# Two-layer hybrid trunk on one core: the feed-forward up projections as Strassen 2x2 block products, the down projection in five parts

## Chip, core and metric

One core of one Trainium2 chip (trn2). The time is the device time of one execution in microseconds (us), the median of the runs shown.

## What is computed

The trunk has two layers on 512 tokens of width D = 1024, and each layer has two feed-forward sublayers (FF = 2816) with a mixer sublayer between them. Four times, therefore, the kernel computes a gated feed-forward step:

```python
def rmsnorm(x, g):
    y = xf * lax.rsqrt(jnp.mean(xf * xf, axis=-1, keepdims=True) + EPS)
    return (y * g).astype(x.dtype)
def swiglu(x, w13, w2):
    g, u = jnp.split(x @ w13, 2, axis=-1)
    return (jax.nn.silu(g) * u) @ w2
...
for l in range(DEPTH):
    x = x + 0.5 * swiglu(rmsnorm(x, ffn1_norm[l]), ffn1_w13[l], ffn1_w2[l])
    h = rmsnorm(x, mix_norm[l])
    ...
    x = x + merged @ w_out[l]
    x = x + 0.5 * swiglu(rmsnorm(x, ffn2_norm[l]), ffn2_w13[l], ffn2_w2[l])
return rmsnorm(x, final_norm)
```

The mixer sublayer (pooling, mLSTM, differential attention) is the same in both kernels.

## The kernel before, in words

Activations are stored feature-major: `x` is 8 tiles of 128 features x 512 tokens. A matmul has a 128x128 weight block as its stationary operand and up to 512 token columns moving past it. Inputs are float32, and each product is made of three matmuls on rounded halves (`k3`, L217, lines L220 to L222): high x high, high x low, low x high. So one output block of an up projection (128 columns of w13, 8 blocks of K) takes 8 x 3 = 24 matmuls of 128x512, and a column pair (gate g and up u) takes 48.

**Weights.** `weight()` (L202) hands out the next weight tile. It is loaded by a DMA on SP's queue (`load_weight`, up to 128x1024 numbers), its high half is cast on ACT (L198) and its low half is a subtract on DVE (L199). The raw tile has 3 buffers, the halves 2 each; loads run two tiles ahead and splits one.

**A feed-forward layer** (`ffn`, L497). The 22 column pairs come in three `PARTS` of 8, 7 and 7. A pair is two blocks, g then u. When g is done, `take_g` multiplies by the norm factor R on DVE (L507) and applies Silu on ACT (L508). When u is done, `take_u` multiplies by R on DVE (L511), forms u*g on POOL (L512), casts the high half on ACT (L514) and subtracts the low half on DVE (L515). After each part come 8 down blocks, one for each 128 output features: as many k steps as the part has pairs, then an update of x on DVE (L531). In the last part each updated x tile is also prepared for the next norm by `prep` (L305): ACT and DVE make `xh` and `xl` = x times the gain, split in halves (L319, L320), ACT squares x (L332) and POOL adds the squares up (L333).

**The norm.** `norm()` (L352) runs beside the first blocks of the stage that follows. It sums the squares over features on PE (L349), takes the power -1/2 on POOL (L341), spreads the result on PE (L371) and copies it to R on ACT (L361). Blocks that end before R is there keep their results in PSUM until R comes (`self.later`).

**Other pieces.** `tables()` (L411 to L494) makes the cosine and sine tables for the mixer, some 25 DVE and some ACT operations on 128x512 tiles; it is issued as `extra` of the very first feed-forward layer, right after its first part's pairs, before the first 8 down blocks. The last layer ends with `finish` (L1041): the last part's down blocks in two halves of 256 token columns, each with its own sum of squares and final norm.

**Order of work.** PE's order is the order in which the program is written (`manual_schedule` for PE). For DVE, ACT, POOL and SP a scheduler fixes one static order in advance; each engine then works through its queue strictly in that order. `weave` (L280) mixes a second generator (norm, mixers) into PE's stream by an estimated clock; `defer` puts a piece of work at a later point of that clock.

```python
PARTS = ((0, 8), (8, 15), (15, 22))
...
    for m in range(KD):
        def take(ps, m=m):
            nc.vector.scalar_tensor_tensor(
                out=self.x[m], in0=ps, scalar=0.5, in1=self.x[m], op0=ALU.mult, op1=ALU.add
            )
            if last:
                self.prep(m, gnext)
        yield from self.fm(act, take)
```

## Time and profile before

| | |
|---|---|
| median of 3 runs | 2309.61 us (2306.61 to 2311.46) |
| profiled execution | 2309.4 us, its span 2307.6 us, mean granted clock 0.992 |
| PE (matmul) busy | 2269.6 us, 98% of the span, 10740 matmuls |
| DVE / ACT / POOL busy | 1236.2 us (54%) / 802.5 us (35%) / 339.5 us (15%) |
| DMA | 220.59 MB, mean 96 GB/s |

The span runs from the first to the last recorded instruction of one profiled execution; 1.8 us of its 2309.4 us lie outside the span. PE's busy share says how much of the span a matmul was in flight. The order of work decides which of the other engines' operations PE waits for, and the list of PE's waits names them.

### The profile page before, as it was taken

How to read it: one execution, taken by the hardware profiler on the slowest of the kernel's cores; microseconds unless marked ns; L12 is line 12 of the kernel's file. 1: busy time of each engine (PE TensorE's matmuls, PEld its weight loads, DVE VectorE, ACT ScalarE, POOL GpSimd, SP SyncE). 2: the span in 40 equal slices, each digit the busy share in tenths (PEclk: the TensorE clock that was granted, in tenths of full speed). 3: DMA queues.
4: the chain of work that ended last, by engine and by line, in shares of the span. 5: the costliest groups of instructions: out<-in, count | busy, mean ns of one | idle time of the engine just before them, and what ended most of it. 6: DMA issues, size and time to landing. Idle time of an engine off the chain costs nothing.

```text
span 2307.6 us, 26698 instructions
## 1 busy us (share of the span) xinstructions
PE 2269.6 (98%) x10740; PEld 1881.1 (82%) x10740; DVE 1236.2 (54%) x1594; ACT 802.5 (35%) x1181; POOL 339.5 (15%) x251
## 2 busy tenths in 40 slices
PE   8999999999999999999999999999999999999998
PEld 6888888887887888888888888888877878888888
DVE  5564455668547454444444444466776564545355
ACT  3332234534353322222332222354334533323234
POOL 3101012012004210101210010110120042101013
PEclk9999999999999999999999999999999999999999
DMA  4333333323222233333333333332322323333334
GB/s 144 103 101 95 97 94 90 102 78 95 86 83 84 90 101 94 98 94 98 97 95 97 95 91 101 92 96 89 92 87 78 87 87 93 99 94 95 100 94 140
DMA packets 67277, 220.59 MB, mean 96 GB/s; under 512 B 8233, under 2 KB 10809, under 8 KB 67153
## 3 DMA queue, kind: packets, MB, share of 16 engines
q1 hardware_dynamic: 64432, 215.86, 31.2%
q10 hardware_dynamic: 2496, 2.43, 0.3%
q8 instruction: 84, 1.38, 0.2%
q0 software_dynamic: 224, 0.60, 0.1%
q14 instruction: 41, 0.33, 0.0%
HBM read 212.55 MB, written 2.11 MB: 93 GB/s over the span
## 4 chain that ended last, share of the span: by engine, by line
PE 88%; DVE 5%; POOL 3%; issue 2%; ACT 2%; DMA 0%; POOLq 0%; SPq 0%; ACTq 0%; DVEq 0%
PE mm L220 28%; PE mm L221 28%; PE mm L222 27%; POOL t L1026 2%; DVE wl L199 1%; PE mx L141 1%; PE mx L138 1%; PE mx L971 1%; PE mx L871 1%; PE mx L541 1%; DVE t L1022 1%; POOL t L512 1%; ACT wh L198 1%; DVE A L562 0%; ACT A L1028 0%
## 5 line engine op out<-in xcount | busy, mean ns | idle before, releaser
L220 PE MATMUL mm<-xh,wh 128*128 128x512 f32 x2080 | 821.8, 395 | 2.0 <-ACT wh L198 1.3
L221 PE MATMUL mm<-xl,wh 128*128 128x512 f32 x2080 | 811.4, 390 | 2.7 <-DVE xl L320 2.6
L222 PE MATMUL mm<-xh,wl 128*128 128x512 f32 x2080 | 812.0, 390 | 0.5 <-DVE wl L199 0.5
L198 ACT CAST wh<-wr 128x1024 fp32r<-128x1024 f32 (+2 forms) x406 | 417.8, 1029 | 1091.5 <-PE mm L221 556.8
L199 DVE TENSOR_TENSOR wl<-wr,wh 128x1024 fp32r<-128x1024 f32 (+2 forms) x406 | 585.7, 1443 | 81.8 <-ACT wh L198 77.3
L221 PEld LDWEIGHTS mm<-xl,wh 128*128 128x128 f32 x2080 | 391.4, 188 | 84.3 <-DVE xl L320 5.9
L222 PEld LDWEIGHTS mm<-xh,wl 128*128 128x128 f32 x2080 | 391.2, 188 | 83.8 <-DVE wl L199 1.3
L220 PEld LDWEIGHTS mm<-xh,wh 128*128 128x128 f32 x2080 | 391.5, 188 | 82.9 <-DVE xh L317 1.9
L220 PE MATMUL mm<-A,wh 128*128 128x512 f32 (+1 forms) x888 | 336.8, 379 | 8.4 <-ACT A L1028 6.8
L221 PE MATMUL mm<-A,wh 128*128 128x512 f32 (+1 forms) x888 | 336.9, 379 | 1.8 <-DVE A L515 1.6
L222 PE MATMUL mm<-A,wl 128*128 128x512 f32 (+1 forms) x888 | 336.2, 379 | 0.6 <-DVE wl L199 0.6
L512 POOL TENSOR_TENSOR t<-t,t 128x512 f32<-128x512 f32 x88 | 119.8, 1361 | 1143.5 <-ACT wh L198 974.8
L511 DVE TENSOR_TENSOR t<-mm,R 128x512 f32<-128x512 f32 x88 | 60.9, 692 | 284.2 <-PE mm L222 284.2
L220 PEld LDWEIGHTS mm<-A,wh 128*128 128x128 f32 x888 | 168.9, 190 | 40.4 <-ACT A L1028 7.6
L221 PEld LDWEIGHTS mm<-A,wh 128*128 128x128 f32 x888 | 169.0, 190 | 35.3 <-DVE A L515 3.8
L222 PEld LDWEIGHTS mm<-A,wl 128*128 128x128 f32 x888 | 168.8, 190 | 31.9 <-DVE wl L199 1.5
L531 DVE SCALAR_TENSOR_TENSOR x<-mm,x 128x512 f32<-128x512 f32 x88 | 60.8, 691 | 215.7 <-PE mm L222 215.7
L507 DVE TENSOR_TENSOR t<-mm,R 128x512 f32<-128x512 f32 x88 | 60.9, 692 | 162.9 <-PE mm L222 147.9
L514 ACT CAST A<-t 128x512 fp32r<-128x512 f32 x88 | 54.8, 622 | 119.9 <-POOL t L512 119.9
L333 POOL TENSOR_TENSOR ssq<-ssq,t 128x512 f32<-128x512 f32 x42 | 70.8, 1685 | 158.8 <-ACT t L332 158.3
L220 PE MATMUL mm<-wh,xh 128*128 128x256 f32 (+1 forms) x256 | 73.7, 288 | 4.2 <-DVE mif L591 2.6
L221 PE MATMUL mm<-wl,xh 128*128 128x256 f32 (+1 forms) x256 | 72.5, 283 | 0.0
(202 smaller groups left out, 1622.7 us busy)
## 6 DMA issues: line engine op xcount, KB each, us to landing
wr<-in_w13a SPq DMA_DIRECT2D x88, 512.0 KB, 3.6
wr<-in_w13b SPq DMA_DIRECT2D x88, 512.0 KB, 3.6
wr<-in_w_fm SPq DMA_DIRECT2D x76, 512.0 KB, 3.6
wr<-in_w2b SPq DMA_DIRECT2D x40, 448.0 KB, 3.3
wr<-in_w2a SPq DMA_DIRECT2D x32, 448.0 KB, 3.3
wr<-in_w2a SPq DMA_DIRECT2D x16, 512.0 KB, 3.7
wr<-in_w_p SPq DMA_DIRECT2D x16, 512.0 KB, 3.5
wr<-in_w_out SPq DMA_DIRECT2D x16, 512.0 KB, 3.5
```

The costliest lines, as they stand in the source:

```text
L198: self.last_hi = nc.scalar.copy(hi, raw)
L199: self.last_lo = nc.vector.tensor_tensor(out=lo, in0=raw, in1=hi.bitcast(F32), op=ALU.subtract)
L220: nc.tensor.matmul(ps, wh, xh, start=start, stop=False)
L221: nc.tensor.matmul(ps, wh, xl, start=False, stop=False)
L222: nc.tensor.matmul(ps, wl, xh, start=False, stop=stop)
L333: nc.gpsimd.tensor_tensor(out=self.ssq, in0=self.ssq, in1=sq, op=ALU.add)
L507: nc.vector.tensor_tensor(out=g, in0=ps, in1=self.R, op=ALU.mult)
L511: nc.vector.tensor_tensor(out=u, in0=ps, in1=self.R, op=ALU.mult)
L512: self.last_pool = nc.gpsimd.tensor_tensor(out=u, in0=u, in1=g, op=ALU.mult)
L514: nc.scalar.copy(ah, u)
L531: nc.vector.scalar_tensor_tensor(out=self.x[m], in0=ps, scalar=0.5, in1=self.x[m], op0=ALU.mult, op1=ALU.add)
L1026: nc.gpsimd.tensor_tensor(out=acc, in0=acc, in1=t, op=ALU.add)
```

## The change

The 22 pairs come in five parts of 5, 5, 4, 4 and 4. The first part's 5 pairs are computed as before. The other 17 pairs of each layer (68 in all four) are computed as a 2x2 block product: K in two halves of 512, the tokens in two halves of 256 (`H`), and the two "rows" of the block are the pair's g and u columns. Instead of 8 products of half blocks there are 7, each 4 k steps x 3 = 12 matmuls of 128x256: 84 matmuls of 128x256 take the place of 48 of 128x512.

The operands of the 7 products are combinations. On the token side `operands(k)` makes x times gain times R (here R is multiplied in before the matmul), the differences t1 to t4 and their high and low halves, all on DVE and ACT, in four calls per layer that come 1, 8, 15 and 22 us of the estimated clock after R. On the weight side `split_weight` makes sums and differences of the raw halves of g and u on DVE (forms f2, f3, f4; f1 is u's raw first half), then splits them as before. The products run in the order a, c, d, b (`pair_a` to `pair_b`); each half result is copied out of PSUM on ACT or added to a copy on DVE, and u*g of these pairs is on DVE (it stays on POOL in the 5 plain pairs). `gated` makes the activation's halves as L514 and L515 did.

The 8 down blocks of part p-1 (5 or 4 k steps each) are laid between the pieces of part p's pairs, in an order that `ffn_plan` sets; the last part's own 8 follow at the end (or the two halves of `finish`). `tables()` is issued where the plan has "x", ahead of the first layer's last 8 down blocks.

Memory changes with it: weights share a ring "w" of 7 tiles, the forms have 7 tiles "V", down weights have tiles "dr", "dh", "dl" of their own, "A" grows from 24 to 52 buffers and takes over xh, xl, y, dv and the squares; pools with a phase replace t2, t4 and mv. Weights are loaded up to 16 us ahead by estimated PE time, and split up to 7 us ahead.

The diff, cut to its core:

```diff
-PARTS = ((0, 8), (8, 15), (15, 22))
+PARTS = ((0, 5), (5, 10), (10, 14), (14, 18), (18, 22))
+H = T // 2
+MM = 0.2268
+def ffn_plan(end):
+    plan = [("u", 0, j) for j in range(*PARTS[0])]
...
+    for p in range(1, n):
+        f0, f1 = PARTS[p]
+        rest = [("D", p - 1, m) for m in range(KD)]
+        tail = [rest.pop() for _ in range(2)][::-1] if p == n - 1 else []
+        slots = 2 * (f1 - f0) - 1
+        put = [[] for _ in range(slots + 1)]
+        for i, d in enumerate(rest):
+            put[1 + i * slots // len(rest)].append(d)
+        for i, j in enumerate(range(f0, f1)):
+            plan += [("a", p, j)] + ([("b", p, j - 1)] if j > PARTS[1][0] else []) + put[2 * i]
+            plan += [("c", p, j)] + put[2 * i + 1] + [("d", p, j)]
+        if p == n - 1:
+            plan += [("b", p, f1 - 1)] + tail
+    plan.append(("x", 0, 0))
+    plan += [("E", n - 1, h) for h in range(2)] if end else [("D", n - 1, m) for m in range(KD)]
+    return plan
...
+            if kind == "f2":
+                raw = src["s"] = self.wtile()
+                add(raw[:, q1], g[:, q1], g[:, q2], ALU.add)
+                add(raw[:, q2], raw[:, q1], u[:, q1], ALU.subtract)
+            elif kind == "f3":
+                raw = u
+                add(u[:, q1], u[:, q1], g[:, q1], ALU.subtract)
+            else:
+                raw = g
+                add(g[:, q1], u[:, q2], src["s"][:, q2], ALU.subtract)
+            hi, lo = self.forms_tile(), self.forms_tile()
+            self.split(hi, lo, raw)
...
+    def operands(self, k, gcol):
...
+            nc.vector.scalar_tensor_tensor(out=xn[:, q], in0=self.x[i], scalar=g, in1=self.R, op0=ALU.mult, op1=ALU.mult)
...
+        for o, a, b in ((t1, b12, b11), (t2, b22, t1), (t3, b22, b12), (t4, b21, t2)):
+            nc.vector.tensor_tensor(out=o, in0=a, in1=b, op=ALU.subtract)
+        v = self.act(dt=F32R)
+        X["b11"][k] = v[:, :H], v[:, H:]
+        self.split(v[:, :H], v[:, H:], b11, False)
+        for src, names in ((xn[:, q2], ("b21", "b22")), (t[:, q1], ("t1", "t2")), (t[:, q2], ("t3", "t4"))):
+            hi, lo = self.act(dt=F32R), self.act(dt=F32R)
+            self.split(hi, lo, src, False)
...
+    def block(self, ps, w, name, start=False):
+        for k, x in enumerate(self.X[name]):
+            self.k3(ps, (w[0][:, k, :], w[1][:, k, :]), x, start and k == 0, k == 3, True)
+            yield 1.5 * MM
+    def gated(self, u, g, act):
+        ah, al = self.act(dt=F32R), self.act(dt=F32R)
+        nc.scalar.copy(ah, u)
+        nc.vector.tensor_tensor(out=al, in0=u, in1=ah.bitcast(F32), op=ALU.subtract)
...
+    def pair_a(self):
+        p = {"a": self.ps("mx")[:, :H], "b": self.ps("mx")[:, :H], "u": self.act(), "g": self.act()}
+        w = self.weight()
+        yield from self.block(p["a"], w, "b11", start=True)
+        nc.scalar.copy(p["u"][:, :H], p["a"])
+        hi, lo = self.weight()
+        yield from self.block(p["b"], (hi[:, 0:4, :], lo[:, 0:4, :]), "t1", start=True)
+        nc.scalar.copy(p["g"][:, H:], p["b"])
...
+    def pair_b(self, p, act):
+        yield from self.block(p["a"], p["a22"], "t4")
+        u, g = p["u"], p["g"]
+        self.last_silu = nc.scalar.activation(g[:, :H], p["a"], AF.Silu)
+        nc.vector.tensor_tensor(out=u, in0=u, in1=g, op=ALU.mult)
+        self.gated(u, g, act)
+    def pair_c(self, p):
+        yield from self.block(a, p["s2"], "t2")
+        nc.scalar.copy(p["u"][:, H:], a)
+        hi, lo = self.weight()
+        ps = self.ps()[:, :H]
+        yield from self.block(ps, (hi[:, 4:8, :], lo[:, 4:8, :]), "b21", start=True)
+        nc.vector.tensor_tensor(out=p["u"][:, :H], in0=p["u"][:, :H], in1=ps, op=ALU.add)
...
+    def pair_d(self, p):
+        yield from self.block(a, p["s3"], "t3")
+        nc.vector.tensor_tensor(out=g[:, H:], in0=g[:, H:], in1=a, op=ALU.add)
+        self.last_silu = nc.scalar.activation(g[:, H:], g[:, H:], AF.Silu)
+        hi, lo = self.weight()
+        yield from self.block(p["b"], (hi[:, 4:8, :], lo[:, 4:8, :]), "b22")
+        nc.vector.tensor_tensor(out=u[:, H:], in0=u[:, H:], in1=p["b"], op=ALU.add)
+        p["a22"] = hi[:, 4:8, :], lo[:, 4:8, :]
...
-            if extra is not None:
-                extra()
-                extra = None
...
+            elif kind == "x":
+                if extra is not None:
+                    extra()
```

The order of the work at two places, as the two kernels' queues have it.

ACT's queue in the first feed-forward layer, around the end of a plain pair. Before (`t2_72` is u of a plain pair, `wh` high halves of weights):

```order
L198 CAST wh_78_365<-wr_73_330 128x1024
L508 ACTIVATE t2_71_328<-t2_71_328 128x512
L198 CAST wh_86_404<-wr_77_363 128x1024
L514 CAST A_81_396<-t2_72_329 128x512
L198 CAST wh_90_437<-wr_85_402 128x1024
L508 ACTIVATE t2_83_400<-t2_83_400 128x512
L198 CAST wh_98_476<-wr_89_435 128x1024
```

With the change (`V_133` holds g and u of the fifth plain pair, `mx_147` and `mx_148` are the first two half results of the first Strassen pair, `w_...` and `V_...` weights and forms):

```order
L264 CAST V_139_605<-w_136_574 128x512
L662 ACTIVATE V_133_569<-V_133_569 128x512
L264 CAST V_141_611<-w_140_608 128x1024
L264 CAST V_151_653<-w_136_574 128x1024
L264 CAST V_158_707<-w_137_576 128x1024
L651 CAST A_145_644<-V_133_569 128x512
L677 COPY A_149_650<-mx_147_648 128x256
L680 COPY A_150_651<-mx_148_649 128x256
L264 CAST V_161_725<-w_155_661 128x512
L264 CAST V_164_762<-w_163_759 128x1024
L697 COPY A_149_650<-mx_147_648 128x256
```

Before, only casts of later weights and the next pair's Silu stand behind the cast of a pair's gated result (L514). Now the two copies out of PSUM (L677, L680) of the first Strassen pair stand behind that cast (L651) in the same queue.

DVE's queue around `tables()`. Before, between two updates of x at the end of the first part (`y_...` are the tables' tiles):

```order
L463 TENSOR_SCALAR y_154_788<-y_153_785 128x512
L464 TENSOR_SCALAR y_154_788<-y_154_788 128x512
L467 SCALAR_TENSOR_TENSOR y_153_785<-y_154_788,y_153_785 128x512
L463 TENSOR_SCALAR y_155_789<-y_153_785 128x512
L474 TENSOR_SCALAR y_156_790<-y_154_788 128x512
L464 TENSOR_SCALAR y_155_789<-y_155_789 128x512
L531 SCALAR_TENSOR_TENSOR x1_2_69<-mm_167_858,x1_2_69 128x512
L199 TENSOR_TENSOR wl_170_887<-wr_164_852,wh_169_886 128x1024
L467 SCALAR_TENSOR_TENSOR y_153_785<-y_155_789,y_153_785 128x512
```

With the change, at the end of the first feed-forward layer (`A_576` to `A_580` are the tables' tiles, L440 makes xl for the mixer stage, L741 updates x, L265 makes a low half of down weights):

```order
L440 SCALAR_TENSOR_TENSOR A_595_3587<-x1_8_78,vec_15_85,A_594_3586 128x512
L612 SCALAR_TENSOR_TENSOR A_579_3510<-A_580_3511,A_579_3510 128x512
L440 SCALAR_TENSOR_TENSOR A_602_3614<-x2_9_79,vec_15_85,A_601_3613 128x512
L265 TENSOR_TENSOR dl_618_3673<-dr_599_3597,dh_617_3672 128x512
L624 TENSOR_TENSOR A_576_3505<-A_576_3505,A_579_3510 128x512
L440 SCALAR_TENSOR_TENSOR A_609_3641<-x3_10_80,vec_15_85,A_608_3640 128x512
L612 SCALAR_TENSOR_TENSOR A_576_3505<-A_580_3511,A_576_3505 128x512
L628 TENSOR_SCALAR A_579_3510<-A_577_3508 128x512
L612 SCALAR_TENSOR_TENSOR A_576_3505<-A_578_3509,A_576_3505 128x512
L612 SCALAR_TENSOR_TENSOR A_579_3510<-A_578_3509,A_579_3510 128x512
L612 SCALAR_TENSOR_TENSOR A_576_3505<-A_577_3508,A_576_3505 128x512
L612 SCALAR_TENSOR_TENSOR A_579_3510<-A_580_3511,A_579_3510 128x512
```

Before, `tables()` shared DVE's queue with updates of x and weight halves alone; now the same operations stand between the updates of x and the xl tiles which the next stage reads first.

## Rows read from the trace of the kernel before

**Rows 1.** Page, busy time of the engines: us, share of the span, instructions.

```profile
PE 2269.6 (98%) x10740; PEld 1881.1 (82%) x10740; DVE 1236.2 (54%) x1594; ACT 802.5 (35%) x1181; POOL 339.5 (15%) x251
```

**Rows 2.** Page, chain that ended last, shares of the span by engine.

```profile
PE 88%; DVE 5%; POOL 3%; issue 2%; ACT 2%; DMA 0%; POOLq 0%; SPq 0%; ACTq 0%; DVEq 0%
```

**Rows 3.** Waits of PE: line, what it waited for, us, times, longest us.

```profile
PE mm L220 <- DVE mif L591: 2.6, 2, 1.3
...
PE mm L220 <- ACT A L514: 1.6, 1, 1.6
```

**Rows 4.** Windows: us, busy time of each engine (instructions), granted clock, DMA share.

```profile
160.00:260.00 100.00, 99.79 (x441) 82.29 (x440) 46.61 (x46) 27.35 (x33) 9.94 (x7) 1.00 0.33 96
424.00:432.00 8.00, 8.00 (x69) 8.00 (x68) 7.16 (x13) 1.95 (x3) 0.00 (x0) 1.00 0.32 74
```

**Rows 5.** Timeline of PE, 128x512 matmuls: start, duration (51 pitches apart).

```profile
2240.00 0.39 PE L222 MATMUL mm<-xh,wl 128*128 128x512 f32 x1
...
2251.56 0.39 PE L222 MATMUL mm<-xh,wl 128*128 128x512 f32 x1
```

**Rows 6.** Timeline of PE, 128x256 matmuls (60 pitches apart).

```profile
424.74 0.28 PE L221 MATMUL mm<-wl,xh 128*128 128x256 f32 x1
...
431.94 0.28 PE L221 MATMUL mm<-wl,xh 128*128 128x256 f32 x1
```

**Rows 7.** Timeline of DVE, ACT and POOL at the end of two pair blocks.

```profile
307.98 0.69 DVE L511 TENSOR_TENSOR t<-mm,R 128x512 f32<-128x512 f32 x1 [3.35 <-PE mm L222]
308.84 1.29 POOL L512 TENSOR_TENSOR t<-t,t 128x512 f32<-128x512 f32 x1 [9.59 <-ACT wh L198]
308.88 2.33 DVE L199 TENSOR_TENSOR wl<-wr,wh 128x1024 fp32r<-128x1024 f32 x1 [0.21 <-ACT wh L198]
310.17 0.62 ACT L514 CAST A<-t 128x512 fp32r<-128x512 f32 x1 [1.32 <-POOL t L512]
...
314.28 1.22 DVE L199 TENSOR_TENSOR wl<-wr,wh 128x1024 fp32r<-128x1024 f32 x1 [0.17 <-ACT wh L198]
```

**Rows 8.** Timeline of DVE and ACT on 256 columns.

```profile
2256.97 0.42 DVE L1051 SCALAR_TENSOR_TENSOR x<-mm,x 128x256 f32<-128x256 f32 x1 [0.59 <-PE mm L222]
2257.69 0.41 ACT L1053 ACTIVATE y<-x 128x256 f32<-128x256 f32 x1
```

**Rows 9.** Timeline of POOL and PE before the split output columns.

```profile
2252.84 2.15 POOL L512 TENSOR_TENSOR t<-t,t 128x512 f32<-128x512 f32 x1 [9.59 <-ACT wh L198]
...
2253.82 0.28 PE L222 MATMUL mm<-A,wl 128*128 128x256 f32 x1
2255.70 0.38 PE L220 MATMUL mm<-A,wh 128*128 128x256 f32 x1 [1.60 <-ACT A L514]
```

**Rows 10.** Windows there: PE, PEld, DVE, ACT, POOL, clock.

```profile
2258.00:2260.00 2.00, 2.00 (x11) 2.00 (x11) 0.91 (x1) 0.51 (x2) 0.00 (x0) 0.50 0.09 17
2260.00:2262.00 2.00, 2.00 (x14) 2.00 (x14) 1.03 (x2) 1.26 (x2) 0.24 (x1) 0.68 0.68 220
```

**Rows 11.** Timeline of ACT, start of the first feed-forward layer.

```profile
33.35 0.59 ACT L361 COPY R<-mx 128x512 f32<-128x512 f32 x1 [4.42 <-PE mx L371]
```

**Rows 12.** Timeline of DVE during tables(), with its first and last row.

```profile
114.02 0.43 DVE L443 TENSOR_TENSOR y<-y 128x256 f32<-128x256 f32 x1 [1.94 <-DMA y<-in_lam]
...
125.52 0.68 DVE L531 SCALAR_TENSOR_TENSOR x<-mm,x 128x512 f32<-128x512 f32 x1
126.12 0.68 DVE L479 TENSOR_TENSOR y<-y,y 128x512 f32<-128x512 f32 x1
...
134.77 0.49 DVE L491 TENSOR_SCALAR sin<-y,const 128x512 f32<-128x512 f32 x1 [0.70 <-ACT y L490]
```

**Rows 13.** Groups by line and shape: count, busy us, mean ns, idle before.

```profile
L531 DVE SCALAR_TENSOR_TENSOR x<-mm,x 128x512 f32<-128x512 f32 x88 | 60.8, 691 | 215.7 <-PE mm L222 215.7
L320 DVE SCALAR_TENSOR_TENSOR xl<-x,vec,xh 128x512 fp32r<-128x512 f32 x48 | 39.5, 830 | 0.1
L1055 POOL TENSOR_TENSOR y<-y,t 128x256 f32<-128x256 f32 x12 | 13.3, 1112 | 20.5 <-ACT t L1053 20.4
```

More of the change, by code (lines that the diff above doesn't have):

```diff
@@ L157, in ffn @@
         def ffn(w13, w2, end=False):
-            for f0, f1 in PARTS:
-                for j in range(f0, f1):
-                    w.extend((w13[j, 0], w13[j, 1]))
-                for _ in range(2 if end and f1 == NF else 1):
-                    w.extend(w2[m, :, f0:f1, :] for m in range(KD))
+            for kind, p, j in ffn_plan(end):
+                f0, f1 = PARTS[p]
+                if kind == "u":
+                    w.extend([("p", w13[j, 0]), ("p", w13[j, 1])])
+                elif kind == "a":
+                    pair = {"g": w13[j, 0], "u": w13[j, 1]}
+                    w.extend([("f1", pair), ("f2", pair)])
+                elif kind == "c":
+                    w.append(("f3", pair))
+                elif kind == "d":
+                    w.append(("f4", pair))
+                elif kind == "D":
+                    w.append(("d", w2[j, :, f0:f1, :]))
+                elif kind == "E":
+                    w.extend(("d", w2[m, :, f0:f1, :]) for m in range(KD))
         for l in range(L):
@@ L364, in norm @@
             done()
+        if gcol is not None:
+            self.X = {n: [None] * 4 for n in ("b11", "b21", "b22", "t1", "t2", "t3", "t4")}
+            for k in range(4):
+                self.defer(1.0 + 7.0 * k, lambda k=k: self.operands(k, gcol))
     def spread(self, rT):
@@ L602, in values @@
             elif i == 1:
-                self.dv = self.t([P, NB, 512], "dv", 1)
+                self.dv = [self.act() for _ in range(NB)]
             def take(b, ps):
@@ L1094, in run @@
     def run(self):
+        self.phase("ffn")
+        self.ffn_memory()
         self.setup()
         for l in range(L):
-            self.weave(self.norm(5.2 if l else 10.4), self.ffn(l * V_L + V_MIX, self.tables if l == 0 else None))
-            self.y = [self.t([P, T], "y", KD) for _ in range(KD)]
+            self.weave(self.norm(5.2 if l else 10.4, gcol=l * V_L + V_FFN1), self.ffn(l * V_L + V_MIX, self.tables if l == 0 else None))
+            self.phase(f"mix{l}")
+            self.y = [self.act() for _ in range(KD)]
             self.weave(self.mixers(l), self.mix_stream(l))
```

224 lines of the change are left out of this document (156 added, 68 removed).

## The prediction

> **What bounds the kernel now.** First the page's busy times: PE's matmuls are in flight for 98% of the span, DVE works for 54% of it, ACT for 35%, POOL for 15% [rows 1]. Then the chain of waits: 88% of it is PE [rows 2], and the list of PE's waits is short; its entries are of the size of 1 to 7 us in all [rows 3]. So the time is the number of matmuls times their pitch, plus little. The windows show how much room the others have: in a steady stretch of column pairs DVE is busy for 46.6 us of 100 and ACT for 27.4, the clock is granted in full, and DMA is a third busy [rows 4]. What the change is worth is therefore read from the pitch of the two sizes of matmul, and what it can lose is read from the places where PE would start to wait. All sums stand against the profiled execution, 2309.4 us; the median of the runs is 2309.6, so one sum serves both. About 0.2% (4.6 us) is what a measurement of this kernel can tell from no change.
>
> **Pairs, the gain.** From 2240.00 to 2251.56 lie 51 pitches of 128x512 matmuls, 0.2267 us each [rows 5]. From 424.74 to 431.94 lie 60 of 128x256, 0.1200 each [rows 6]. Half the columns thus cost 53%, not 50%: 2 x 0.1200 - 0.2267 = 0.0133 is fixed in each matmul. A plain pair is 48 x 0.2267 = 10.88 us, a Strassen pair 84 x 0.1200 = 10.08, so a pair gains 0.80 and 68 pairs gain **54.4 us**. The seventh product saved is worth an eighth, and nearly half of that is lost on the fixed part. Bounds: 0.1134 for a matmul (exactly half) would give 92; 0.125 would give 26. I take the measured pitch: same tile sizes, a weight load for every matmul, full clock.
>
> The Trainium skill (TensorE: Matmul & The Clock Gate, Back-to-back issue gap) gives 262 cycles for 256 columns and 518 for 512, a fixed part of 6 cycles. By that the pairs would gain about 81 us. The rows here show a fixed part some five times as large, and the sum goes by them.
>
> The last layer's two halves have 8 x 4 x 3 matmuls of 256 columns each instead of 8 x 7 x 3; the rest of that work moves into blocks of 512. That is 144 fewer at 0.1200 for 72 more at 0.2267: 17.28 - 16.32, **-0.9 us**. Down blocks elsewhere are the same matmuls in five parts, so zero.
>
> **The start.** Two of the first blocks and the sum of squares run before R as now; the first squares keep POOL as long as before. I take zero, between -3 and +3.
>
> **From plain pairs to the first Strassen pair (four times).** The first piece of a pair is two products, 24 x 0.12 = 2.88 us, and the next (t2) accumulates in the PSUM of the first, so it waits until ACT has copied that out (L677). In ACT's queue this copy stands behind L651, the cast of the fifth plain pair's u*g, which waits for POOL, which waits for DVE. From the start of DVE's multiplication to the end of ACT's cast the same chain took 310.79 - 307.98 = 2.81 us [rows 7]. With a copy of 256 columns (0.41, as in [rows 8]) that is 3.22, and PE would wait 0.4. With POOL at 2.15 us instead of 1.29, as when it met busy neighbours [rows 9], it is 4.1, and with the hand-overs PE waits some 1.6. I take **1.6**, for DVE is busy with operands there. PE stops of such length were followed in one case by a half-rate stretch: after the stop of 1.60 us at 2255.70 the granted clock is 0.50 for 2 us and 0.68 for the next 2, some 3.3 us at half rate, 1.6 lost [rows 9, 10]; the stops of 1.3 at L591 [rows 3] left the clock alone. Half that loss is 0.8.
>
> In the first layer R comes late, at 33.35 [rows 11], in the third of ten plain blocks, so about 7.5 blocks x 5.44 = 41 us are left until Strassen begins. DVE has to do there: ten multiplications by R (0.69, 6.9 us), five low halves (3.4), seven weight halves (1.15, 8.0) of which five meet POOL's u*g, where the subtract took 2.33 instead of 1.22 [rows 7] (5.5), the first forms (3.1), and four calls of `operands`: in each two products (pitch 0.60 in [rows 12]), four differences of 256 columns and a low half (0.42 in [rows 8]) and three low halves of 512, about 5 us, 20 in all. That is 47 against 41. I take **5.1** of waiting and the loss of clock behind it, 6.7. In the other three layers `norm` is laid 5.2 instead of 10.4 us of estimated clock into the stage, so their operands fit. Sum: 6.7 + 3 x 2.4 = **+14**. Bounds: 1.6 (four times 0.4) and 27 (all like the first).
>
> **End of the first layer, `tables()`.** Before, it lay between blocks with nothing urgent on DVE: from 114.02 to 135.26, less four updates of x and four weight halves, some 13 us are its own [rows 12]. Now it is issued with the last 8 down blocks, 12 x 0.2267 = 2.72 us each, 21.8 in all. There DVE has 8 times update (0.69), xl (0.83 in the mean) [rows 13] and down-weight half (0.69): 17.7. Together 31 us, so DVE ends 9 late, more where POOL's sums of squares slow it, and the mixer stage's first block reads all eight xl. I take **+10**, between 0 (the queue puts tables behind xl) and 16.
>
> **Smaller waits.** The last pair of the first Strassen part has no down block between c and d, so t3 waits for copies behind a weight cast: 0.4, and 0.15 twice at part borders, **+2.8** over four layers (0 to 6). The last layer's halves now have 1.44 us for a block instead of 2.52, against a POOL add of 1.11 [rows 13] and ACT's cast, square and gain of 1.5 together: **+2.5** (0 to 5). Others **+2** (0 to 4).
>
> **In the middle of the stage: nothing.** A Strassen pair with two down blocks takes 10.08 + 2 x 2.7 = 15.5 us. On DVE stand in it: low halves of the forms (0.6 and three of 1.13), four sums and differences of 512 weights (2.4), three PSUM additions of 256 columns (1.3), u*g and a low half (1.4), two down halves (1.5) and two updates (1.4): 12 us, 77%. ACT has about 7.5, POOL nothing. Taken in queue order, each of PE's waits in the period has at least 3 us of slack, so DVE's work is hidden there. If that cover went, each microsecond too much per pair would cost 68.
>
> **Sum.** -54.4 - 0.9 + 14 + 10 + 2.8 + 2.5 + 2 = -24.0, so 2309.4 - 24.0 = 2285.4, in round numbers **2285 us**.
>
> **Rivals.** *The places of transition are hidden.* Queue order is not time; if operands and `tables()` find gaps, waits shrink to 1.6 + a few, and the time is 2256 to 2266. For it: DVE has 46% idle now. Against it: the sums of 47 on 41 and 31 on 22 us. Chance 0.18.
>
> *DVE becomes the pacer of the Strassen stage (slower).* It decides once DVE's 12 us per pair pass 15.5, when its operations are 1.3 times as long as here. That can come from neighbours, or from waits in its strict queue: a form's low half waits for ACT's cast while an addition out of PSUM that PE needs stands behind it. At 0.9 us too much per pair 68 pairs cost 61: 2285 + 61 = 2346. For it: the subtract of 2.33 beside POOL [rows 7]. Against it: POOL is idle in that stage. Chance 0.13.
>
> *Weight loads no longer fit behind a matmul (slower).* 440 loads show 82.29 us on PE's load unit [rows 4], 0.19 each and more than 0.12; if loads went one by one, a pair would take 84 x 0.19 = 16.0 us, 5.1 more than now, and the kernel some 2309 + 345 = 2654. Against it: in 424 to 432 loads are in flight all of the time (8.00 of 8) and the pitch is still 0.12 [rows 4, 6]. Chance 0.02.
>
> The Trainium skill (TensorE: Matmul & The Clock Gate, What overlaps and what doesn't) says that a weight load overlaps a running matmul only in another row group. All loads here fill the whole array, so it speaks against many short matmuls. The trace does not agree, since the pitch has no room for a load of its own.
>
> *The gain is eaten, no change.* All waits at their upper bounds are 27 + 16 + 6 + 5 + 4 = 58 against the 55.3 gained, 2312. For it: queues that are strict make several waits late together. Against it: five bounds would have to be met at once. Chance 0.07.
>
> **Numbers.** The forecast itself has 0.60: faster, as has the hidden case (0.18), so faster 0.78; same 0.07; slower 0.13 + 0.02 = 0.15. The range runs from the lower bounds of all waits (2309.4 - 55.3 + 1.6, about 2256) to the sum of the upper ones, 2312, which leaves out the two slower cases and little else.
>
> **What would show it.** The pitch of 128x256 in the pairs at 0.120; PE's waits before t2 (L697) of the first pair on ACT's copy; PE's waits in the mixer's first block on xl (L440); no wait in the steady pairs, DVE there at 70 to 80%. Wrong it would be if the pitch in the pairs is over 0.13, or if PE waits in every pair on DVE's forms.

## The result, and the profile after

The changed kernel takes 2285.84 us (median of four runs, 2282.55 to 2287.61) against 2308.69 (2306.61 to 2311.46) for the kernel before on the same chip: ratio 0.9899, 95% interval 0.9882 to 0.9916. Forecast were 2285. The profiled executions are 2286.44 and 2309.4, so the ledger below stands against -23.0 us. One of the runs below, the fourth of `align`, took 4655.56 us, twice as long as the other three, and is left out of its numbers.

The page first: busy times and the chain, which answer to [rows 1, 2].

```profile
span 2284.6 us, 33195 instructions
...
PE 2218.4 (97%) x13116; PEld 1944.4 (85%) x13116; DVE 1581.7 (69%) x2426; ACT 1020.4 (45%) x1717; POOL 234.0 (10%) x183
...
PE 25%; DVE 4%; DMA 1%; ACT 1%; issue 1%; POOL 1%; POOLq 0%; DVEq 0%; ACTq 0%
```

PE has 2376 matmuls more and 51 us less to do, for each product now streams 256 columns. DVE went from 54 to 69% and ACT from 35 to 45%. The chain of this page accounts for a third of the span only and can't be read as the one before; the waits and the stages say more. PE's waits (columns as in [rows 3]):

```profile
PE mx L341 <- ACT A L677: 11.7, 4, 4.1
PE mm L341 <- ACT A L821: 5.8, 2, 2.9
PE mm L341 <- DVE x L741: 3.7, 1, 3.7
...
PE mx L341 <- ACT A L1218: 3.0, 2, 1.6
...
PE mx L342 <- DVE A L1219: 3.0, 4, 1.2
PE mx L469 <- POOL A L1263: 2.9, 1, 2.9
PE mm L342 <- DVE A L652: 2.5, 8, 0.3
```

At the head stands the forecast one: t2 of the first Strassen pair waits until ACT has copied the first product out of PSUM (L677), four times. L741 is `tables()` at the end of the first layer. L821 (copies of the values, dv, out of PSUM) and L1218, L1219 (the casts of the mixer's result and their low halves) are in the mixer stage, which the change doesn't touch and to which I had given nothing.

Where the time went shows best by stage. The borders are the last update of x in each: first feed-forward layer, mixer, second feed-forward, the same three of layer 1. The changed kernel's first border, 381.8, is the start of a row with the last two updates; the very last starts at 382.39. The columns are those of [rows 4]; first the kernel before, then the changed one, whose last row is a steady stretch of Strassen pairs.

```profile
40.00:378.70 338.70, 338.49 (x1493) 280.04 (x1492) 173.11 (x192) 104.02 (x127) 40.24 (x35) 1.00 0.34 99
378.70:792.10 413.40, 403.63 (x2069) 334.90 (x2068) 262.27 (x428) 178.01 (x314) 70.84 (x47) 0.99 0.29 88
792.10:1154.00 361.90, 361.48 (x1601) 298.86 (x1600) 168.23 (x167) 106.93 (x131) 43.73 (x30) 1.00 0.32 96
1154.00:1516.00 362.00, 361.60 (x1602) 299.01 (x1601) 169.01 (x167) 105.79 (x130) 43.83 (x34) 1.00 0.32 96
1516.00:1928.60 412.60, 402.54 (x2069) 334.37 (x2069) 262.69 (x427) 177.67 (x314) 71.40 (x46) 0.99 0.29 88
1928.60:2307.60 379.00, 368.45 (x1793) 312.07 (x1791) 177.59 (x190) 113.38 (x147) 54.51 (x44) 0.99 0.34 102
```

```profile
40.00:381.80 341.80, 331.46 (x2127) 301.40 (x2126) 261.59 (x395) 155.67 (x256) 18.68 (x18) 0.99 0.31 96
381.80:804.30 422.50, 408.35 (x2063) 335.61 (x2062) 266.83 (x435) 183.11 (x322) 66.49 (x48) 0.98 0.27 87
804.30:1151.70 347.40, 345.05 (x2213) 313.53 (x2212) 256.29 (x376) 162.43 (x265) 20.64 (x13) 1.00 0.33 102
1151.70:1503.20 351.50, 346.64 (x2214) 314.93 (x2213) 254.45 (x375) 160.18 (x262) 19.30 (x14) 1.00 0.31 97
1503.20:1919.40 416.20, 404.96 (x2069) 334.53 (x2068) 261.44 (x428) 178.83 (x314) 63.96 (x52) 0.99 0.28 88
1919.40:2284.60 365.20, 351.35 (x2333) 322.43 (x2331) 259.73 (x396) 163.21 (x278) 29.44 (x27) 0.98 0.33 100
...
960.00:1060.00 100.00, 99.69 (x690) 92.67 (x689) 73.17 (x108) 44.66 (x75) 0.00 (x0) 1.00 0.33 101
```

The first feed-forward layer, with its start, lost 3.1 us (378.7 to 381.8), the mixers lost 9.1 and 3.6; the other feed-forward layers gained 14.5, 10.5 and 13.8. In the steady stretch DVE is at 73%, and PE is in flight but for one stop of 0.31 us at a border of two parts (L652): no wait inside a part, as forecast. The pitch there (60 pitches apart, answering to [rows 6]):

```profile
1032.78 0.28 PE L341 MATMUL mx<-A,V 128*128 128x256 f32 x1
...
1039.85 0.40 PE L341 MATMUL mm<-A,dh 128*128 128x512 f32 x1
```

That is 7.07 / 60 = 0.1178 us, not 0.1200. A pair then takes 84 x 0.1178 = 9.90 us instead of 10.88, and 68 pairs gain 67.0, where 54.4 were forecast. Against that stand the transitions. The queues at the first Strassen pair of layer 1 (DVE, POOL, ACT, PE; start, duration; in brackets the idle time before and what ended it):

```profile
1205.15 0.69 DVE L287 TENSOR_TENSOR w<-w 128x512 f32<-128x512 f32 x1 [1.62 <-DMA w<-in_w13a]
...
1211.29 0.68 DVE L287 TENSOR_TENSOR w<-w 128x512 f32<-128x512 f32 x1
1211.89 0.68 DVE L665 TENSOR_TENSOR V<-mm,R 128x512 f32<-128x512 f32 x1
...
1212.74 1.55 POOL L666 TENSOR_TENSOR V<-V 128x512 f32<-128x512 f32 x1 [10.60 <-DVE V L665]
1213.09 2.28 DVE L265 TENSOR_TENSOR V<-w,V 128x1024 fp32r<-128x1024 f32 x1
1214.32 0.62 ACT L651 CAST A<-V 128x512 fp32r<-128x512 f32 x1 [2.96 <-POOL V L666]
1214.85 0.36 ACT L677 COPY A<-mx 128x256 f32<-128x256 f32 x1
1215.26 0.48 PE L341 MATMUL mx<-A,V 128*128 128x256 f32 x1 [4.13 <-ACT A L677]
```

The chain is the one forecast: DVE multiplies u by R (L665), POOL multiplies by g (L666), ACT casts (L651), and the copy that frees the PSUM (L677) comes behind it in ACT's queue. What starts it late is a burst on DVE: sums and low halves of the next pair's weights (L287, L265) stand ahead of L665 from 1205.15 to 1211.97, since those weights had just landed. The clock follows:

```profile
1214.00:1216.00 2.00, 0.74 (x4) 0.74 (x5) 1.97 (x2) 1.16 (x3) 0.29 (x1) 0.85 0.11 43
1216.00:1218.00 2.00, 2.00 (x11) 2.00 (x11) 1.34 (x3) 0.71 (x2) 0.00 (x0) 0.50 0.73 252
...
866.00:868.00 2.00, 2.00 (x19) 2.00 (x19) 1.61 (x3) 1.68 (x3) 0.00 (x0) 1.00 0.79 262
```

After the stop of 4.13 us the granted clock is 0.50 for 2 us (11 matmuls instead of 19); after the one of 1.73 at 865.00 it stays 1.00.

### The profile page after: what moved, and what is told of

Read it like the earlier page. It is cut to its first block, busy times and chain, and to the rows that moved or that the text cites. A ratio compares the mean times of both kernels' runs of the same rounds, so it can differ in the third digit from the quotient of the medians.

```text
span 2284.6 us, 33195 instructions
## 1 busy us (share of the span) xinstructions
PE 2218.4 (97%) x13116; PEld 1944.4 (85%) x13116; DVE 1581.7 (69%) x2426; ACT 1020.4 (45%) x1717; POOL 234.0 (10%) x183
## 5 line engine op out<-in xcount | busy, mean ns | idle before, releaser
L341 PE MATMUL mx<-A,V 128*128 128x256 f32 x1632 | 457.0, 280 | 11.7 <-ACT A L677 11.7
L343 PE MATMUL mx<-A,V 128*128 128x256 f32 x1632 | 457.8, 280 | 1.4 <-DVE V L265 1.3
L341 PE MATMUL mm<-A,w 128*128 128x512 f32 x1120 | 450.9, 403 | 7.2 <-DVE x L741 3.7
L342 PE MATMUL mx<-A,V 128*128 128x256 f32 x1632 | 456.2, 280 | 0.0
L342 PE MATMUL mm<-A,w 128*128 128x512 f32 x1120 | 440.5, 393 | 4.1 <-DVE A L1219 1.9
L343 PE MATMUL mm<-A,w 128*128 128x512 f32 x1120 | 441.0, 394 | 2.0 <-DVE w L265 2.0
L265 DVE TENSOR_TENSOR V<-w,V 128x1024 fp32r<-128x1024 f32 (+1 forms) x272 | 295.5, 1105 | 159.1 <-PE mx L342 96.8
L264 ACT CAST V<-w 128x1024 fp32r<-128x1024 f32 (+1 forms) x272 | 256.5, 943 | 272.3 <-issue 98.0
L341 PEld LDWEIGHTS mx<-A,V 128*128 128x128 f32 x1632 | 306.3, 188 | 17.6 <-ACT A L677 12.5
L342 PEld LDWEIGHTS mx<-A,V 128*128 128x128 f32 x1632 | 307.9, 189 | 4.4
L343 PEld LDWEIGHTS mx<-A,V 128*128 128x128 f32 x1632 | 307.5, 188 | 2.0 <-DVE V L265 2.0
L264 ACT CAST w<-w 128x1024 fp32r<-128x1024 f32 (+2 forms) x166 | 172.4, 1039 | 295.5 <-PE mm L342 94.2
L265 DVE TENSOR_TENSOR w<-w,w 128x1024 fp32r<-128x1024 f32 (+2 forms) x166 | 209.8, 1264 | 107.4 <-ACT w L264 107.0
L342 PE MATMUL mm<-A,dh 128*128 128x512 f32 (+1 forms) x736 | 281.0, 382 | 2.5 <-DVE A L652 2.5
L343 PE MATMUL mm<-A,dl 128*128 128x512 f32 (+1 forms) x736 | 279.9, 380 | 0.9 <-DVE dl L265 0.8
L341 PE MATMUL mm<-A,dh 128*128 128x512 f32 (+1 forms) x736 | 280.6, 381 | 0.0
L341 PEld LDWEIGHTS mm<-A,w 128*128 128x128 f32 x1120 | 213.1, 190 | 52.3 <-ACT w L264 4.2
L342 PEld LDWEIGHTS mm<-A,w 128*128 128x128 f32 x1120 | 213.1, 190 | 49.7 <-DVE A L1219 3.6
L343 PEld LDWEIGHTS mm<-A,w 128*128 128x128 f32 x1120 | 212.2, 189 | 48.1 <-DVE w L265 2.5
L741 DVE SCALAR_TENSOR_TENSOR x<-mm,x 128x512 f32<-128x512 f32 x152 | 104.5, 688 | 121.3 <-PE mm L343 121.3
```

The lines of the kernel that those rows point to most:

```text
L264: self.last_hi = nc.scalar.copy(hi, raw)
L265: self.last_lo = nc.vector.tensor_tensor(out=lo, in0=raw, in1=hi.bitcast(F32), op=ALU.subtract)
L341: nc.tensor.matmul(ps, wh, xh, start=start, stop=False, skip_group_check=more)
L342: nc.tensor.matmul(ps, wh, xl, start=False, stop=False, skip_group_check=more)
L343: nc.tensor.matmul(ps, wl, xh, start=False, stop=stop, skip_group_check=more)
L741: nc.vector.scalar_tensor_tensor(out=self.x[m], in0=ps, scalar=0.5, in1=self.x[m], op0=ALU.mult, op1=ALU.add)
```

## Experiments

In the expectations below, the theories are numbered: 1 that the pitch comes from where the tiles lie, 2 that L677 waits behind L651, 3 that `tables()` is laid too early, 4 that ACT's order in the mixer causes the waits on L821; the rivals bear the same numbers. Each run stands beside runs of the kernel before on the same chip, so ratios are to that kernel, and are to be compared with 0.9899. An edit that adds or drops a line shifts the line numbers behind it: the copy L677 is L678 in `align` and `dve6` and L680 in `copyfirst`, and the cast L651 is L652 in `dve6`.

**The pitch: `pad0`, `A64`, `align`.** A tile of 64 bytes per partition (`pad`) shifts the form tiles V by 64 bytes modulo 128 against A. `pad0` takes it away.

```diff
 self.forms_tile()
-self.t([P, 16], "pad")
 for c in "rhl":
```

> The 64-byte pad between the forms V and the down weights is left out, so that the V tiles start at the same offset modulo 128 bytes of a partition as the A tiles that move past them (in the changed kernel they stand 64 bytes apart). Nothing else changes. Theory 1 (the offset between weight tile and moving tile sets the pitch of the matmuls): 128x256 in the pairs goes from 0.1178 to 0.1200 us, as where both tiles have the same offset before; 68 x 84 x 0.0022 = 12.6 us slower, about 2298. Rival 1 (the pitch is a matter of the order of the products or of the PSUM in use): 0.1178 stays and the time too.

Measured: 2298.06 us (2297.22 to 2300.74), ratio 0.9955 [0.9938, 0.9971], 12.2 slower than the changed kernel. The mean pitch of the pairs' 4700 matmuls that follow without a wait is 0.1198, against 0.1175 in the changed kernel. The 12.6 us that the forecast lacked are thus the work of one small tile.

`A64` puts the 64 bytes before A instead, so that V, w and the down weights dh, dl all lie 64 from A.

```diff
+self.sb.tile([P, 16], F32, name="padA", tag="padA", bufs=1)
 warm = self.act(dt=BF16)
...
-self.t([P, 16], "pad")
```

> All A tiles are moved by 64 bytes, V back to offset 0, so that every weight tile (w, V, dh and dl) now stands 64 bytes apart from the A tiles, modulo 128. Theory 1: the pairs keep 0.1178, and the other blocks, which had tiles of equal offset, get shorter too: the 256-column ones 0.1200 to 0.1178, those of 512 columns by as much at least, 0.2267 to 0.2245 or less; some 5400 matmuls of 512 columns x 0.0022 = 12 us faster, about 2274. Rival 1 (offset plays no role, or only at 256 columns): within 3 us of 2285.

Measured: 2285.35 (2280.56 to 2289.73), 0.9897 [0.988, 0.9915], no different from the changed kernel. Pairs went on falling, to 0.1166 in the mean, but the blocks of 512 columns rose. Forty pitches of plain blocks, first in `A64`, then in the changed kernel:

```profile
840.20 0.39 PE L340 MATMUL mm<-A,w 128*128 128x512 f32 x1
...
849.35 0.39 PE L341 MATMUL mm<-A,w 128*128 128x512 f32 x1
```

```profile
840.11 0.39 PE L342 MATMUL mm<-A,w 128*128 128x512 f32 x1
...
849.18 0.39 PE L343 MATMUL mm<-A,w 128*128 128x512 f32 x1
```

9.15 / 40 = 0.2288 against 9.07 / 40 = 0.2268. The sign turns with the tile size, and the sum comes to nothing; I had expected both sizes to gain.

`align` shifts A's partners the other way: w, A, dh, dl at 64, V at 0. The distances are those of the changed kernel, the absolute places are swapped.

```diff
+self.sb.tile([P, 16], F32, name="padW", tag="padW", bufs=1)
 self.load_weight(0)
...
-self.t([P, 24], "pad2")
+self.t([P, 8], "pad2")
```

> w, A, dh and dl all at offset 64 modulo 128 bytes of a partition, V at 0. Theory 1a (the offset of the moving tile counts by itself at 256 columns, the distance of both at 512, as the kernel with A alone moved had 0.1166 in the pairs but 0.2292 for 512 columns): pairs 0.1166, 512 columns back at 0.2278; 5700 x 0.0011 = 6 us faster, about 2279. Rival 1a (a moving tile at offset 64 makes 512 columns slow whatever the weights' offset): 0.2292 stays and the time is that of the changed kernel, 2285.

Measured: 2292.92 (median of three, 2292.05 to 2294.40), 0.9936 [0.9916, 0.9956]. The pitches are those of the changed kernel (0.1175 and 0.2278 in the mean), so both expectations fall: with the places swapped and the distance kept, the pitch stays. The distance doesn't explain all, for V and A have the same places in `A64` as in `align`, and the pairs had 0.1166 there; that is open. The time is 7 us longer for another reason: the waits on the copy rose from 11.7 to 16.1, and the reduced clock (reckoned as under `copyfirst`) from 27.7 to 34.8.

```profile
PE mx L341 <- ACT A L678: 16.1, 4, 5.3
```

**The copy behind the cast: `copyfirst`, `ufirst`.** `copyfirst` lays the fifth plain pair's `gated()` (L651, L652) behind the first piece of the first Strassen pair, so that L677 and L680 come first in ACT's queue.

```diff
-            self.gated(u, g, act)
+            if late:
+                self.late = lambda: self.gated(u, g, act)
+            else:
+                self.gated(u, g, act)
...
                 pairs[j] = yield from self.pair_a()
+                if j == PARTS[1][0]:
+                    self.late()
```

> The cast of the fifth plain pair's u*g (gated, L651, L652) is written behind the first Strassen pair's piece a, so that ACT has the two copies out of PSUM (L677, L680) ahead of it. Theory 2 (t2 waits because the copy stands behind a cast that waits for POOL and DVE): PE's four waits on L677, 11.7 us in all, go, and with them the half-rate stretches behind the two of 4.1 (1.7 us each): 13 to 15 us faster, about 2271, unless the cast is late for the first down block. Rival 2 (the operands of the first layer are late, the copy only carries the wait): in the first layer's ups a wait of 3 to 5 us comes back on a V or A tile of DVE, and 4 to 8 us are gained.

Measured: 2268.65 (2268.22 to 2275.92), 0.9833 [0.9817, 0.9849], 17.2 faster than the changed kernel. The four waits of 4.1, 1.7, 4.1, 1.7 are gone; two of half a microsecond are left, on the same copy:

```profile
80.69 0.39 PE L341 MATMUL mx<-A,V 128*128 128x256 f32 x1 [0.56 <-ACT A L680]
...
1200.81 0.38 PE L341 MATMUL mx<-A,V 128*128 128x256 f32 x1 [0.55 <-ACT A L680]
```

Waits fell by 10.6 us there. Summing (1 - granted clock) x 2 us over all windows of 2 us gives 23.2 us of reduced clock instead of 27.7, another 4.5. This is theory 2, shown.

`ufirst` asks why the wait is 4.1 twice and 1.7 twice: it orders one sum of the next pair's forms behind L665 of the fifth pair.

```diff
-                nc.vector.tensor_tensor(out=out, in0=in0, in1=in1, op=op)
+                i = nc.vector.tensor_tensor(out=out, in0=in0, in1=in1, op=op)
+            if self.last_u is not None and kind == "f3":
+                self.order(i, self.last_u)
+                self.last_u = None
```

> The changed kernel with one order added on DVE: the forms f3 of the first Strassen pair come behind the multiplication of the fifth plain pair's u by R (L665). The copies stay behind the cast. Theory 2a (L665 stands behind four operations on the forms in DVE's queue, whose weights landed late, so the whole chain to the copy is late in the first feed-forward layers): the waits on L677 shrink from 4.1 to about 1.5 there, from 1.7 to about 1 in the others, with the half-rate stretches: 8 to 10 us faster, about 2277. Rival 2a (the forms are then late instead): PE waits on V by as much, and the time stays near 2285.

Measured: 2286.80 (2284.05 to 2287.97), 0.9906 [0.9893, 0.992]. The waits became 3.35, 2.37, 2.85 and 1.95: the long ones shrank, the short ones grew, the sum went from 11.7 to 10.5. So the burst of form operations is part of the difference between 4.1 and 1.7, not all of it; the rest stays open. The 2277 of theory 2a was missed: the time is that of rival 2a, but without its reason, for PE waits no longer on V (1.1 instead of 1.3).

**The plan without Strassen: `planonly`.** The five-part order of down blocks stays, all pairs are plain.

```diff
-            plan += [("a", p, j)] + ([("b", p, j - 1)] if j > PARTS[1][0] else []) + put[2 * i]
-            plan += [("c", p, j)] + put[2 * i + 1] + [("d", p, j)]
+            plan += put[2 * i] + [("g", p, j)] + put[2 * i + 1] + [("v", p, j)]
...
-            for k in range(4):
-                self.defer(1.0 + 7.0 * k, lambda k=k: self.operands(k, gcol))
```

> All 22 pairs plain, in five parts with the down blocks laid between the pairs, no operands and no forms; tables() still ahead of the last 8 down blocks. It tells the plan from the products. By the sum of the prediction: -0.9 for the halves of 256, +10 for tables(), +2.5 for the last layer's halves, so 2309 + 12 = 2321, and the Strassen products are then worth 36 us net. Rival (the plan itself gains): below 2309.

Measured: 2335.31 (2333.91 to 2336.11), 1.0114 [1.0099, 1.0129], 14 above what I expected. The new plan alone costs 26 us, and the products give back 2335.3 - 2285.8 = 49.5: the 67.0 of the pitch less about 16 at the transitions. By stages, the two middle feed-forward layers are as before (722.5 against 723.9 together). The loss is in the first layer (391.5 against 378.7, +12.8) and in the mixers (423.5 and 418.9 against 413.4 and 412.6, +10.1 and +6.3). So the mixers' loss doesn't come from the products. `planonly` keeps the changed kernel's memory and its distances for loading and splitting weights, so which part of the new plan brings the loss isn't shown.

**The end of the first layer: `tabend`.** `tables()` behind the last eight down blocks instead of ahead of them.

```diff
-    plan.append(("x", 0, 0))
     plan += [("E", n - 1, h) for h in range(2)] if end else [("D", n - 1, m) for m in range(KD)]
+    plan.append(("x", 0, 0))
```

> tables() is issued behind the first layer's last 8 down blocks instead of ahead of them, so that updates of x and the xl tiles come first in DVE's queue. Theory 3 (tables() makes DVE late at the end of the first layer): the waits there (3.7 on x, 1.7 on xl, 0.6 on dl, 0.4 on the sums) and the half-rate stretches around 380 and 390 us (5.1 us lost) go: 10 to 12 us faster, about 2275. Rival 3 (DVE has no room in the mixer stage either): the wait moves behind the border, 0 to 5 us are gained.

Measured: 2285.75 (2282.62 to 2287.00), 0.9901 [0.9887, 0.9916]: nothing. As rival 3 has it, the wait moved: the last update of x in the first layer started at 374.0 instead of 382.4, but in the mixer PE then waited for results that DVE takes out of PSUM behind the tables' operations in its queue (3.40 on L766 at 403.17, 4.35 on L801 at 418.49), and the waits on L677 rose from 11.7 to 15.5, as in `align`. With the edit of `copyfirst` (`cf_tab`) those are out of the way:

> copyfirst and tabend together: the copies out of PSUM ahead of the late cast, and tables() behind the last 8 down blocks. In the kernels so far the wait on L677 came out in two sizes, 4.1 or 5.3 us, whatever was changed elsewhere, and hid what tabend gained (its first layer and mixer took 6.8 us less by the profile). Theory 3: without that wait the gain shows, 2268.7 less 5 to 8, about 2262. Rival 3: the waits on L766 and L801 in the mixer eat it, 2268.

2269.35 (2268.70 to 2271.66), 0.9834 [0.9821, 0.9847], no gain over `copyfirst` either, with the same two waits (3.40 and 4.34). At neither of the two places tried do the 13 us of tables stand where nobody waits.

**The mixers: `dvfirst`.** In the changed kernel ACT's order has the exponential L1047, with its table load, ahead of the four copies L821:

```profile
1567.79 1.28 ACT L1047 ACT_TABLE_LOAD   x1
1569.08 0.21 ACT L1047 ACTIVATE g_thr<-g_thr 128x16 f32<-128x16 f32 x1
1569.21 1.55 ACT L821 ACTIVATE A<-mm,rT 128x256 f32<-128x256 f32 x4
```

Before, three of the copies (there L611) came first, each as its block was done:

```profile
1575.06 0.48 ACT L611 ACTIVATE dv<-mm,rT 128x256 f32<-128x256 f32 x1 [1.32 <-PE mm L222]
1576.44 0.47 ACT L611 ACTIVATE dv<-mm,rT 128x256 f32<-128x256 f32 x1 [0.90 <-PE mm L222]
1577.88 0.47 ACT L611 ACTIVATE dv<-mm,rT 128x256 f32<-128x256 f32 x1 [0.96 <-PE mm L222]
...
1580.92 1.28 ACT L837 ACT_TABLE_LOAD   x1
```

`dvfirst` orders the exponential behind the last copy.

```diff
-        nc.scalar.activation(thr, thr, AF.Exp, scale=-1.0)
+        te = nc.scalar.activation(thr, thr, AF.Exp, scale=-1.0)
+        if self.last_dv is not None:
+            self.order(te, self.last_dv)
```

> In each mixer the Exp of mlstm_gates (L1047), which waits for a chain on DVE, is ordered behind the copies of the values out of PSUM (L821) that stood behind it in ACT's queue. Theory 4 (the mixers lose time because the scheduler's order of ACT changed there): PE's two waits of 2.9 us on L821 and the half-rate stretches behind them (1.7 us lost each) go: 8 to 9 us faster, about 2277. Rival 4 (the chain behind the Exp is what PE needs next): PE waits later in the same stage and nothing is gained.

Measured: 2286.27 (2281.68 to 2286.73), 0.9901 [0.9886, 0.9916], no change in all. PE's two waits on these copies fell from 2.90 to 1.39, and the mixers gained 4.0 and 2.9 us (418.6 and 413.4 instead of 422.6 and 416.3), but the waits on L677 rose from 11.7 to 14.5 in all, as much as 5.27 at once, and took part of it back. With `copyfirst`, where those are gone (`cf_dv`):

> copyfirst and dvfirst together. By the profile of dvfirst its two mixers took 4.0 and 2.9 us less than in the changed kernel. Theory 4: 2268.7 less 7, about 2262. Rival 4: the gain was chance in one profile, 2268.

2267.63 (2265.43 to 2269.30), 0.9824 [0.9811, 0.9838]. The waits on the copies are 1.39 here too, but against `copyfirst`'s own mixers (420.2 and 415.9) these are shorter by only 1.1 and 1.9 (419.1 and 414.0), and the gain of 1.0 us in all lies within the scatter. That the two waits come from the order on ACT is shown by their halving; that this is worth the 6.9 us of the stages is not.

**Room on DVE: `dve6`.** One sum of the forms is written seven times instead of once, 3.6 us of DVE more per pair, with the same result.

```diff
-                add(raw[:, q1], g[:, q1], g[:, q2], ALU.add)
+                for _ in range(7):
+                    add(raw[:, q1], g[:, q1], g[:, q2], ALU.add)
```

> The first sum of the weight forms is computed seven times over instead of once in every Strassen pair: 6 more DVE operations of 512, 6 x 0.60 = 3.6 us a pair, the same result. It prices the cover of DVE in the steady pairs: 11.3 us of 15.5 there now, 14.9 with it. Theory 5 (at least 3 us of slack at each wait): the steady pairs do not change by more than 0.3 us each (20 us in all), and only the places of transition get 3 to 6 us longer; 2290 to 2310. Rival 5 (DVE's strict queue paces PE already close to this load): over 1 us a pair, above 2350.

Measured: 2389.18 (2385.25 to 2392.11), 1.0351 [1.0335, 1.0366], +103 of the 68 x 3.6 = 245 us added. That is far above the 2290 to 2310 of theory 5 and in the range of rival 5. But its reason, a delay in every pair, isn't what the trace shows. Inside a part the pairs still run without a wait, with DVE at 90% (59.99 of 67.00); the 2.78 us that PE lacks in this row are the wait at its end, at a border of parts:

```profile
990.00:1057.00 67.00, 64.22 (x444) 59.51 (x442) 59.99 (x90) 28.45 (x47) 0.00 (x0) 1.00 0.28 90
```

The loss stands at the borders, from PE's timeline:

```profile
896.81 0.58 PE L342 MATMUL mx<-A,V 128*128 128x256 f32 x1 [7.82 <-ACT A L678]
...
1056.91 0.49 PE L342 MATMUL mm<-A,dh 128*128 128x512 f32 x1 [2.78 <-ACT A L652]
```

6.6 to 7.8 us at the first pair, with 21.7 us on late forms V around it, 12 waits of 2.5 to 3.7 at the borders of parts, and 77.5 us of reduced clock in all instead of 27.7. So the 3.6 us were hidden within a part and were not at its border. DVE is no pacer in the changed kernel.

**The sum: `cf_all`.** The edits of `copyfirst`, `tabend` and `dvfirst`, and the first two casts of down weights ordered behind the squares at the start:

```diff
             self.split(hi, lo, raw, i > 1)
+            if kind == "d" and i < 24:
+                self.order(self.last_hi, self.last_sq)
```

> copyfirst, tabend and dvfirst together, and the casts of the first two down weights ordered behind the squares at the start (they stood ahead of them in ACT's and DVE's queues, and the sum of squares, R and so PE were late by some 3 us, with a half-rate stretch). If the parts add up: 2268.7 - 6 - 7 - 4, about 2252; if each wait only gives way to the next, 2262.

Measured: 2262.92 (five runs, 2258.84 to 2266.81), 0.9808 [0.9795, 0.9822]: the fastest version, 23 us below the changed kernel and 45 below the one before. 17.2 of the 23 are `copyfirst`'s; the rest is less sure, since the intervals of the two kernels overlap. The time is the 2262 of waits that give way to the next, not the 2252 of parts that add up. In its profiled execution (2258.84) the reduced clock is 18.1 us, as before the change (18.0). The first layer ends at 367.1, 7 earlier than in `tabend`, and the waits behind the tables' operations are still there (3.40 and 4.55). The effects of the edits don't add: what one removes, the next wait in line takes up in part.

## Why the prediction was right

The time is within 1 us of the forecast, but the terms are not: two errors of some 12 us have cancelled. The mechanisms were right in the main; that the total is so close is luck.

| term | forecast | measured |
|---|---|---|
| pairs | -54.4 | -67.0 |
| last layer's halves | -0.9 | -0.9 (their pitch is still 0.1200) |
| start | 0 | +3.4 |
| to the first Strassen pair | +14 | +16.4 |
| `tables()` | +10 | +11.5 |
| smaller waits | +2.8 | +2.5 |
| the split output | +2.5 | +1.5 |
| others, mixers | +2 | +7.3 |
| sum | -24.0 | -25.3 |

Measured in all are -23.0, so 2.3 us are assigned to nothing. Start and mixers came out above the upper bounds given for them (3 and 4).

*Pairs: mis-sized.* The term "I take the measured pitch: same tile sizes, a weight load for every matmul" was 12.6 us short. Equal sizes were not enough for an equal pitch: [rows 6] show tiles with the same place modulo 128 bytes, and the change lays V 64 bytes off. `pad0` gave the forecast's pitch and 12.2 us back. The Trainium skill (TensorE: Matmul & The Clock Gate, Back-to-back issue gap) states a fixed part of 2.5 ns, the prediction's 6 cycles, for a matmul by itself. The traces don't agree at either distance: with tiles at the same place it is 2 x 0.1200 - 0.2267 = 0.0133 us, and in `A64`, where all stand 64 bytes apart, 2 x 0.1166 - 0.2292 = 0.0040 us by the means. The section says nothing of the place of the tiles.

*Start: a zero that wasn't.* "The first squares keep POOL as long as before" left out when they begin. R comes at 36.67 instead of 33.35, and the granted clock is 0.50 from 28 to 34 us. POOL's sums of the squares, in the kernel before, in the changed one and in `cf_all`:

```profile
8.44 11.41 POOL L333 TENSOR_TENSOR ssq<-ssq,t 128x512 f32<-128x512 f32 x7 [7.11 <-ACT t L332]
...
15.75 12.51 POOL L453 TENSOR_TENSOR ssq<-ssq,A 128x512 f32<-128x512 f32 x7 [14.49 <-ACT A L452]
...
14.67 13.30 POOL L455 TENSOR_TENSOR ssq<-ssq,A 128x512 f32<-128x512 f32 x7 [13.41 <-ACT A L454]
```

They take about as long but begin 7.3 us later, because ACT now has all but the first square behind casts of weights and the halves of x. By the expectation of `cf_all`, two casts of down weights ahead of the squares made R late. That isn't so: these casts took 1.33 us together, and with them behind the squares POOL's sums end at 27.97 instead of 28.26, PE still waits 3.10 us for them (2.72 in the changed kernel), and R comes at 35.15, against 35.40 in `copyfirst`, which lacks the edit. No run moves the squares themselves, so that cause is read from the queue and not tested.

*First Strassen pair: size and place right, one reason wrong.* 16.4 is four waits (11.7), two stops of 1.3 together before them (L265) and twice 1.7 of clock. The mechanism, copy behind cast behind POOL behind DVE, is what `copyfirst` took away. But the step "47 against 41" for the first layer alone fails: layer 1's first feed-forward shows the same 4.13, though its operands were done and DVE stood idle for 1.62 us just before the burst. In the first layer too the last operation on the operands ends at 73.1, before the burst begins, and DVE then stands idle for 1.83 us. The forecast of 1.6 for layer 1 came out at 4.13; 1.73 and 1.70 fit the other two.

*Tables: right.* PE waits 3.74 us on L741 at 378.69, 1.7 on xl (L440), some 1 on smaller things, and loses 5.1 by the clock; the sum was forecast as 10. `tabend` adds that the one other place tried doesn't save it.

*Mixers: the term left out.* "Others +2" was meant for them and for all else. By the stages they lost 12.7 us, of which 5 to 6 are the tables' cost behind the first border, so the 7.3 is good to about half a microsecond. It is a net figure, for PE's waits of 3.4 (twice) and 2.4 (twice) in the mixers before are gone or smaller. The new plan shifts what comes in ACT's and DVE's queues after it. The waits of 2.90 on L821 (at 453.62 and 1569.71), with 1.7 us of reduced clock after each, are the largest part. In layer 1 the casts L1218 also stand behind a weight cast that waited 3.81 us for its DMA (1826.17). `planonly` shows that the plan brings the loss.

*The middle: right inside a part.* No wait at 73%, and `dve6` shows 3.6 us of further room there. "At each of PE's waits" is too much: at the borders of parts PE already waits 0.31 eight times (L652), so there the room is nil, which `dve6` shows as 2.5 to 3.7.

*Rivals.* The pacer's condition was not met (73%); weight loads were hidden at 0.1178 as at 0.1200; the hidden case was not met, and that `cf_all` lies in its band of 2256 to 2266 doesn't bear it out: the band was reckoned with 54.4 for the pairs, and with the measured 67.0 it would be 2243 to 2253.

## What to carry to other kernels

When pieces of work get smaller, look at the places where one kind of work follows the other: the steady part gave what the pitch promised, and a quarter of it was lost at four seams, nearly all of which one moved cast won back (17.2 us, with the clock). A measured pitch holds for tiles that lie as the measured ones did; with a matmul of 0.12 us, a tile of 64 bytes was worth 12 us. Any new order also moves queues in stages that the diff doesn't name, so their waits belong into the sum.
